# Keeping the low halves of weight blocks in DRAM between the two token halves of a two-block transformer kernel

## Chip, cores and metric

The kernel runs on one NeuronCore of a Trainium2 chip. The metric is the device time of one execution in microseconds, as the median of several runs. Engine names are those of the profile: PE (TensorE, with PEld for its weight loads), DVE (VectorE), ACT (ScalarE), POOL (GpSimd), SP (SyncE, which here only issues transfers).

## What is computed

512 tokens of width 1024 go through two blocks of a transformer, in float32. The first block has two layers: layer 0 is pooling beside latent attention, layer 1 is differential attention; each is followed by a SwiGLU feed-forward of width 2816. The second block has a mixer (stick-breaking attention, a gated linear recurrence, attention to a memory) and an expert layer that picks 16 experts per head for 8 heads. Cut to what matters here:

```python
def swiglu(h, w_gate, w_up, w_down):                 # D_MODEL 1024, D_FF 2816
    return (jax.nn.silu(h @ w_gate) * (h @ w_up)) @ w_down

def peer_ffn(h, w_query, sub_keys, expert_u, expert_v):
    q = (x_blk @ w_query).reshape(b, t, PEER_HEADS, 2, HALF_KEY)    # 1024 x 2048 weights
    scores = jnp.einsum('bthcd,hcnd->bthcn', q, sub_keys)
    top_s, top_i = lax.top_k(scores, PEER_TOPK)
    ...

# first block, layer 1:   h = h + diff_block(...);  h = h + swiglu(rmsnorm(h), ...)
# second block:           x = x + mixed @ w_out;    x = x + peer_ffn(rms_norm(x), ...)
```

## The kernel before

Every product is made of three matmuls (`mm3`, lines 268 to 271). A float32 operand is split into a high part, rounded to the matmul's format, and a low part, the rest. The three matmuls take high by high (line 269), high weight by low input (line 270) and low weight by high input (line 271), and add up in PSUM. `split` (lines 230 to 232) makes the two parts: ACT copies into the rounded format (line 231), and DVE or POOL subtracts (line 232).

`load_w` (lines 247 to 266) brings a weight block of 1024 x 256 in two parts of 128 partitions x 1024 columns: a transfer on SP's queue into `raw` (line 256, three buffers), then the split into `whi` and `wlo` (three buffers each). A second list, `LO`, says which engine subtracts each of the two parts. `low(n)` (lines 243 to 245) sets it: 0 means DVE for both parts, 2 means POOL for both, 1 means POOL for the first and DVE for the second. A part's buffers come free when its matmuls have run; the order of buffers follows the order of the program.

In the feed-forward of layer 1 the tokens are processed in two halves of 256, by two generators made by `ffn1` (lines 922 to 958): `ffn_a` for the first half and `ffn_b` for the second. Both load and split the same weights anew through `ffn` (lines 502 to 548): 11 gate blocks (line 527), 11 up blocks (line 530) and 12 down blocks (line 538; in the last of three rounds a part is 768 columns wide). The 8 query blocks of the expert layer (`queries`, line 1434) are likewise loaded for each half, in `PA.queries()` and `PB.queries()`.

The order around the change is written by hand at lines 1352 to 1361, 1720 to 1730 and 1763 to 1767, with generators that run side by side at given rates; a list scheduler then orders each engine's instructions by a model of time, so that an engine's queue is not simply the program's order. In time the stages are:

- 830 to 1047 us: `ffn_a` beside `memory()`, with `low(LO_A)`, which is `low(0)`.
- 1047 to 1134 us: projections of the first half for the mixer, with `low(2)`.
- 1134 to 1320 us: the mixer of the first half beside `ffn_b`, with `low(2)`. The mixer's recurrence (lines 1146 to 1226) alternates small DVE products with small matmuls (line 1170).
- 1320 to 1560 us: the mixer's output, `PA.queries()` beside the rest of `ffn_b`, with `low(2)`, then `low(LO_Z)`, which is `low(1)`, for the end of `ffn_b` (from about 1500 us) and the projections of the second half. `route` and `decode` (lines 1449 to 1512) run top-16 searches and one-hot products on DVE.
- 1560 to 1770 us: the mixer of the second half.
- 1770 to 2085 us: `PB.queries()` beside scores against expert rows (`scores`, line 1620, which also uses `load_w`) and gathers of expert rows by POOL-issued transfers (line 1516), whose scores DVE makes (line 1530), with `low(LO_P)`, which is `low(1)`.
- 2085 us to the end: the rest of the scores and the experts' sum.

The instructions that the prediction's steps touch are the subtraction at line 232, the ACT copy at line 231, the transfer at line 256, the matmul at line 271 that needs the low part, and on DVE lines 1479, 1496 and 1499 (`route` and `decode`).

Of the kernel before, what the change touches and what calls it, by code (L numbers as in the profile page):

```python
# [9 lines left out]
F = mybir.dt.float32  # L10
FR = mybir.dt.float32r
# [3 lines left out]
AF = mybir.ActivationFunctionType  # L15
# [6 lines left out]
S, D, KT = 512, 1024, 8  # L22
# [9 lines left out]
RB, WB = 3, 3  # L32
U2, UZ, UD = 3, 3, 4
LO_A, LO_Y, LO_M, LO_Z, LO_P = 0, 2, 2, 1, 1
# [18 lines left out]
F_1, F_2, F_3, F_4, L_4 = 1, 36, 2, 20, 1  # L53
# [114 lines left out]
def interleave(*gens):  # L168
    for _ in side_by_side(*gens):
        pass  # L170


def alongside(main, *others):

    live = [[g, n, 0] for g, n in (main,) + others]
    while True:
        e = min(live, key=lambda e: e[2] / e[1])
        e[2] += 1
        try:
            next(e[0])  # L180
        except StopIteration:
            if e[0] is main[0]:
                return
            live.remove(e)
# [7 lines left out]
def build(tc, A, out, stop=None, dump=None):  # L192
    nc = tc.nc
    V, SC, PE, GP = nc.vector, nc.scalar, nc.tensor, nc.gpsimd
    ctx = ExitStack()
    with ctx:
# [4 lines left out]
        tmps = ExitStack()  # L201
        tmp = tmps.enter_context(tc.tile_pool(name="tmp", bufs=2))
        psum = ctx.enter_context(tc.tile_pool(name="psum", bufs=8, space=PSUM))

        def ps(w=S):
            t = psum.tile([128, S], F, name="ps")
# [23 lines left out]
        def split(hi, lo, src, eng=V):  # L230
            SC.activation(hi, src, AF.Copy)  # L231
            eng.tensor_sub(lo, src, hi.bitcast(F))  # L232
# [10 lines left out]
        def low(n):  # L243

            LO[:] = [GP] * n + [V] * (2 - n)

        def load_w(ap, kt, eng=LO):

            n = ap.shape[1]
            w = n // kt  # L250
            half = (kt + 1) // 2
            parts = []
            for i, (a, b) in enumerate(((0, half), (half, kt))):
                c = (b - a) * w
                raw = wp.tile([128, 1024], F, name="raw", bufs=RB)[:, :c]
                nc.sync.dma_start(raw, ap[:, a * w:b * w])
                hi = wp.tile([128, 1024], FR, name="whi", bufs=WB)[:, :c]
                lo = wp.tile([128, 1024], FR, name="wlo", bufs=WB)[:, :c]
                split(hi, lo, raw, eng[i])
                parts.append((hi, lo))  # L260

            def get(k):
                hi, lo = parts[k >= half]
                k -= half if k >= half else 0
                return hi[:, k * w:(k + 1) * w], lo[:, k * w:(k + 1) * w]
            return get
# [235 lines left out]
        def ffn(l, nm, xh, xl, w, sl_, ah, al, stile, after):  # L502

            for r, (f0, nf, kd) in enumerate(FF_ROUNDS[l]):
                a_hi, a_lo = ah(), al()
                gates = []

                def gate_out(p):
                    s = stile()
                    V.tensor_mul(s, p, nm.R)  # L510
                    i = SC.activation(s, s, AF.Silu)
                    gates.append(s)
                    if MIXING[0] and len(gates) % 2 == 0:
                        in_order(i)
                        exp_ln()

                def up_out(f):
                    def ev(p):
                        u = stile()
                        V.tensor_mul(u, p, nm.R)  # L520
                        V.tensor_mul(u, u, gates.pop(0))
                        split(a_hi(f), a_lo(f), u)
                    return ev

                def items():
                    for c in range(nf // 2):
                        wg = load_w(A["w_gate%d" % l][f0 // 2 + c], KT)
                        yield lambda: feat_mm(ps(w), wg, 0, xh, xl), gate_out, True
                        yield lambda: feat_mm(ps(w), wg, 1, xh, xl), gate_out
                        wu = load_w(A["w_up%d" % l][f0 // 2 + c], KT)  # L530
                        yield lambda: feat_mm(ps(w), wu, 0, xh, xl), up_out(2 * c), True
                        yield lambda: feat_mm(ps(w), wu, 1, xh, xl), up_out(2 * c + 1)

                yield from steps(items(), {H_F[l][0]: [nm.roots], H_F[l][1]: [nm.rows]} if r == 0 else {})
                for c in range(4):
                    pp = [ps(w) for _ in range(2)]
                    for q in range(nf // kd):
                        wd = load_w(A["w_down%d%d" % (l, r)][c, q], kd)
                        for m in range(2):
                            for k in range(kd):  # L540
                                h, lo = wd(k)
                                f, mc = q * kd + k, slice(m * 128, m * 128 + 128)
                                mm3(pp[m], h[:, mc], lo[:, mc], a_hi(f), a_lo(f), f == 0, f == nf - 1)
                            yield
                    for m in range(2):
                        V.tensor_add(X[:, 2 * c + m, sl_], X[:, 2 * c + m, sl_], pp[m])
                    if r == len(FF_ROUNDS[l]) - 1:
                        after(2 * c + 2)
# [801 lines left out]
            between_inner(h.q0)  # L1350

        low(LO_A)
        interleave((ffn_a, 36), (memory(), 24))
        low(LO_Y)
        alongside((projections(HA), 16), (ffn_b, F_1))
        open_mix()
# [20 lines left out]
        hp = hps.enter_context(tc.tile_pool(name="rows", bufs=1, side="right"))  # L1377
        routes = ExitStack()
        RP = {}
        dram = ctx.enter_context(tc.tile_pool(name="dram", bufs=1, space=bass.MemoryType.DRAM))  # L1380
        Gd = dram.tile([4 * NV, 128, 128, 32], F, name="Gd")
        Sd = [dram.tile([128, 4, 128 * NV], F, name="Sd%d" % g) for g in range(NU)]

# [24 lines left out]
        class Peer:  # L1408
# [20 lines left out]
            def queries(self):  # L1429
                rp = RP[0] = routes.enter_context(tc.tile_pool(name="route", bufs=1, side="right"))  # L1430
                qs = {}
                for hd in range(9):
                    if hd < 8:
                        w = load_w(A["w_query"][hd], KT)
                        qs[hd] = rp.tile([128, 2, W], F, name="qh", bufs=2)
                        pp = [feat_mm(ps(W), w, m, self.xh, self.xl) for m in range(2)]
                        yield
                        for m in range(2):
                            SC.activation(qs[hd][:, m], pp[m], AF.Copy)
                        yield  # L1440
                    if hd == 0:
                        for t in range(self.ng):
                            self.rows(t)
                            yield
                    if hd >= 1:
                        yield from self.route(hd - 1, qs[hd - 1])
                routes.close()
# [272 lines left out]
        gather_a = gathered()  # L1720

        alongside((normed(0, W, xh, xl), 20), (ffn_b, F_3))
        alongside((PA.queries(), 112), (ffn_b, F_4), (gather_a, L_4))
        low(LO_Z)
        for _ in ffn_b:
            pass
        HB = Half(W, big)
        ring[0] = fixed_ring(UZ)
        open_mix()
# [73 lines left out]
```

## Time and profile before

| | |
|---|---|
| median of three runs | 3046.31 us (3045.76 to 10148.63) |
| the profiled execution's own time | 3051.8 us |
| its span | 3050.0 us |
| PE busy | 2886.0 us (95%) |
| DVE busy | 2142.5 us (70%) |
| ACT busy | 1375.8 us (45%) |
| POOL busy | 1155.7 us (38%) |
| granted PE clock, mean | 0.977 |

One execution is profiled, and all durations are from it. "Busy" is the time in which an engine has an instruction; a busy PE may still be waiting inside for weights. The granted clock is a share of full speed. In a row of a group, `out<-in` names what is written and read, `xN` is how many instructions there are, and after the bar stand the time busy and the mean of one in ns. In the waits, the first name waited for the second: us in total, times, longest.

### The profile page before, as it was taken

How to read it: one execution, taken by the hardware profiler on the slowest of the kernel's cores; microseconds unless marked ns; L12 is line 12 of the kernel's file. 1: busy time of each engine (PE TensorE's matmuls, PEld its weight loads, DVE VectorE, ACT ScalarE, POOL GpSimd, SP SyncE). 2: the span in 40 equal slices, each digit the busy share in tenths (PEclk: the TensorE clock that was granted, in tenths of full speed). 3: DMA queues.
4: the chain of work that ended last, by engine and by line, in shares of the span. 5: the costliest groups of instructions: out<-in, count | busy, mean ns of one | idle time of the engine just before them, and what ended most of it. 6: DMA issues, size and time to landing. Idle time of an engine off the chain costs nothing.

```text
span 3050.0 us, 44591 instructions
## 1 busy us (share of the span) xinstructions
PE 2886.0 (95%) x16770; PEld 2540.1 (83%) x16770; DVE 2142.5 (70%) x3877; ACT 1375.8 (45%) x2363; POOL 1155.7 (38%) x718
## 2 busy tenths in 40 slices
PE   8999999999999998889789989989999999899999
PEld 6568888878799998789786688889999998777887
DVE  6854344498776628659975668998787758788753
ACT  4533223477454545444354433337666643333332
POOL 3110000344310285468453146654554534444200
PEclk9999999999999999999899989999999999999999
DMA  3122232321255543245342157777877889999964
GB/s 134 41 77 97 87 107 85 101 70 42 59 179 180 173 159 105 84 137 182 114 153 74 39 197 279 252 261 290 301 287 282 299 318 387 363 373 380 340 224 145
DMA packets 195881, 568.29 MB, mean 186 GB/s; under 512 B 16944, under 2 KB 68528, under 8 KB 194000
## 3 DMA queue, kind: packets, MB, share of 16 engines
q1 hardware_dynamic: 157664, 427.61, 40.4%
q0 software_dynamic: 37712, 137.71, 12.1%
q8 instruction: 132, 2.16, 0.3%
q14 instruction: 85, 0.70, 0.1%
q10 hardware_dynamic: 288, 0.11, 0.0%
HBM read 512.93 MB, written 52.43 MB: 185 GB/s over the span
## 4 chain that ended last, share of the span: by engine, by line
PE 68%; DVE 18%; DMA 6%; ACT 3%; issue 3%; POOL 2%; SPq 0%; ACTq 0%; DVEq 0%; POOLq 0%
PE ps L269 14%; PE ps L271 14%; PE ps L270 14%; PE ps L1682 5%; PE ps L1683 5%; PE ps L1681 5%; PE ps L1563 3%; DVE wlo L232 2%; DMA raw<-in_peer_v_dram 2%; DMA u<-in_peer_u_dram,ix 2%; DVE u L1530 1%; POOL wlo L232 1%; PE ps L487 1%; PE ps L1170 1%; DVE nm L457 1%
## 5 line engine op out<-in xcount | busy, mean ns | idle before, releaser
L232 POOL TENSOR_TENSOR wlo<-raw,whi 128x1024 fp32r<-128x1024 f32 (+2 forms) x236 | 589.2, 2506 | 585.9 <-ACT whi L231 547.8
L231 ACT ACTIVATE whi<-raw 128x1024 fp32r<-128x1024 f32 (+2 forms) x518 | 515.6, 997 | 629.8 <-PE ps L270 344.3
L232 DVE TENSOR_TENSOR wlo<-raw,whi 128x1024 fp32r<-128x1024 f32 (+3 forms) x282 | 357.3, 1269 | 217.2 <-ACT whi L231 212.5
L271 PE MATMUL ps<-yh,wlo 128*128 128x384 f32 (+1 forms) x1152 | 386.0, 336 | 30.3 <-DVE wlo L232 30.2
L269 PE MATMUL ps<-yh,whi 128*128 128x384 f32 (+1 forms) x1152 | 389.8, 339 | 0.0
L270 PE MATMUL ps<-yl,whi 128*128 128x384 f32 (+1 forms) x1152 | 384.2, 334 | 0.0
L1682 PE MATMUL ps<-vl,gh 128*128 128x512 f32 x768 | 302.5, 394 | 3.7 <-DVE vl L232 3.5
L1683 PE MATMUL ps<-vh,gl 128*128 128x512 f32 x768 | 300.8, 392 | 0.0
L269 PE MATMUL ps<-XH,whi 128*128 128x512 f32 (+1 forms) x680 | 270.3, 402 | 8.6 <-ACT whi L231 8.6
L1516 POOL DMA_INDIRECT u<-in_peer_v_dram,ix x128 | 197.3, 1541 | 203.5 <-DVE h L1595 179.0
L270 PE MATMUL ps<-XL,whi 128*128 128x512 f32 (+1 forms) x680 | 267.1, 395 | 0.0
L271 PE MATMUL ps<-XH,wlo 128*128 128x512 f32 (+1 forms) x680 | 262.7, 395 | 1.8 <-DVE wlo L232 1.8
L1681 PE MATMUL ps<-vh,gh 128*128 128x512 f32 x768 | 240.3, 393 | 9.2 <-ACT vh L231 9.2
L271 PEld LDWEIGHTS ps<-yh,wlo 128*128 128x128 f32 x1152 | 219.7, 191 | 35.1 <-DVE wlo L232 35.1
L231 ACT ACTIVATE vh<-raw 128x1024 fp32r<-128x1024 f32 x128 | 133.2, 1055 | 249.7 <-DMA raw<-in_peer_v_dram 174.1
L1530 DVE SCALAR_TENSOR_TENSOR u<-u,h 128x1024 f32<-128x1024 f32 x127 | 185.3, 1465 | 52.3 <-DMA u<-in_peer_u_dram,ix 52.2
L270 PEld LDWEIGHTS ps<-yl,whi 128*128 128x128 f32 x1152 | 220.3, 191 | 0.0
L269 PEld LDWEIGHTS ps<-yh,whi 128*128 128x128 f32 x1152 | 220.1, 191 | 0.0
L369 POOL TENSOR_TENSOR sqa<-sqa,sq 128x512 f32<-128x512 f32 (+1 forms) x28 | 42.5, 1518 | 439.3 <-ACT sq L367 438.4
L269 PE MATMUL ps<-fx,whi 128*128 128x256 f32 x704 | 201.3, 289 | 6.2 <-ACT fx L353 4.4
L271 PE MATMUL ps<-fx,wlo 128*128 128x256 f32 x704 | 196.1, 287 | 5.9 <-DVE wlo L232 3.3
L232 DVE TENSOR_TENSOR vl<-raw,vh 128x1024 fp32r<-128x1024 f32 x128 | 155.3, 1222 | 65.6 <-ACT vh L231 65.2
(428 smaller groups left out, 7124.3 us busy)
## 6 DMA issues: line engine op xcount, KB each, us to landing
raw<-in_uT_dram SPq DMA_DIRECT2D x128, 512.0 KB, 6.0
raw<-in_peer_v_dram SPq DMA_DIRECT2D x128, 512.0 KB, 6.8
raw<-in_w_gate_dram SPq DMA_DIRECT2D x66, 512.0 KB, 3.7
raw<-in_w_up_dram SPq DMA_DIRECT2D x66, 512.0 KB, 3.8
raw<-in_w_in_dram SPq DMA_DIRECT2D x52, 512.0 KB, 3.7
Sd<-s SPq DMA_DIRECT2D x32, 768.0 KB, 6.4
Gd<-st SPq DMA_DIRECT2D x12, 2048.0 KB, 10.5
gt<-Gd SPq DMA_DIRECT2D x32, 768.0 KB, 8.7
```

The costliest lines, as they stand in the source:

```text
L231: SC.activation(hi, src, AF.Copy)
L232: eng.tensor_sub(lo, src, hi.bitcast(F))
L269: PE.matmul(out, wh, xh, start=first, stop=False)
L270: PE.matmul(out, wh, xl, start=False, stop=False)
L271: PE.matmul(out, wl, xh, start=False, stop=last)
L369: GP.tensor_add(self.acc, self.acc, q)
L1516: i = GP.indirect_dma_start(out=u, out_offset=None, in_=A[table], in_offset=bass.IndirectOffsetOnAxis(ap=self.idx[t, hd][:, j:j + 1], axis=0))
L1530: V.scalar_tensor_tensor(u, u, 1.0, self.h2[t], op0=OP.mult, op1=OP.mult, accum_out=self.sd[t][:, hd, j:j + 1])
L1563: PE.matmul(p[:, n * 128:(n + 1) * 128], q[:, n], e[:, n], start=True, stop=True)
L1681: PE.matmul(p, gh[:, e, ts], h[:, cs], start=False, stop=False, skip_group_check=True)
L1682: PE.matmul(p, gh[:, e, ts], l[:, cs], start=False, stop=False, skip_group_check=True)
L1683: PE.matmul(p, gl[:, e, ts], h[:, cs], start=False, stop=end, skip_group_check=True)
```

## The change

In `ffn_a` and in `PA.queries()` the low part of the second half (`i == 1`) of each block is written into a buffer of a pool of its own, three deep, and stored from there to a DRAM tensor by a transfer that POOL issues. In `ffn_b` and in `PB.queries()` the low part of that half is not computed: a transfer on SP's queue loads it from DRAM into a `wlo` buffer, and ACT makes the high part from `raw` as before. Layer 0 and all other weights keep the old way. The numbers: 34 feed-forward and 8 query parts are stored once and loaded once.

```diff
-        def load_w(ap, kt, eng=LO):
+        KEPT, KEEP = {}, [None]
+        def load_w(ap, kt, eng=LO, key=None):
...
                 hi = wp.tile([128, 1024], FR, name="whi", bufs=WB)[:, :c]
-                lo = wp.tile([128, 1024], FR, name="wlo", bufs=WB)[:, :c]
-                split(hi, lo, raw, eng[i])
+                keep = i == 1 and key is not None
+                first = keep and key not in KEPT
+                lo = (KEEP[0]() if first else wp.tile([128, 1024], FR, name="wlo", bufs=WB))[:, :c]
+                if keep and not first:
+                    nc.sync.dma_start(lo.bitcast(F), KEPT[key])
+                    SC.activation(hi, raw, AF.Copy)
+                else:
+                    split(hi, lo, raw, eng[i])
+                if first:
+                    KEPT[key] = dram.tile([128, c], F, name="kept%d" % len(KEPT))
+                    nc.gpsimd.dma_start(KEPT[key], lo.bitcast(F))
...
-                        wg = load_w(A["w_gate%d" % l][f0 // 2 + c], KT)
+                        wg = load_w(A["w_gate%d" % l][f0 // 2 + c], KT, key=("gate", f0 // 2 + c) if l else None)
-                        wu = load_w(A["w_up%d" % l][f0 // 2 + c], KT)
+                        wu = load_w(A["w_up%d" % l][f0 // 2 + c], KT, key=("up", f0 // 2 + c) if l else None)
-                        wd = load_w(A["w_down%d%d" % (l, r)][c, q], kd)
+                        wd = load_w(A["w_down%d%d" % (l, r)][c, q], kd, key=("down", r, c, q) if l else None)
...
-        interleave((ffn_a, 36), (memory(), 24))
+        with tc.tile_pool(name="kept", bufs=1) as kp:
+            KEEP[0] = lambda: kp.tile([128, 1024], FR, name="kl", bufs=3)
+            interleave((ffn_a, 36), (memory(), 24))
...
-                        w = load_w(A["w_query"][hd], KT)
+                        w = load_w(A["w_query"][hd], KT, key=("query", hd))
...
-        alongside((PA.queries(), 112), (ffn_b, F_4), (gather_a, L_4))
-        low(LO_Z)
-        for _ in ffn_b:
-            pass
+        with tc.tile_pool(name="kept2", bufs=1) as kp:
+            KEEP[0] = lambda: kp.tile([128, 1024], FR, name="kl", bufs=3)
+            alongside((PA.queries(), 112), (ffn_b, F_4), (gather_a, L_4))
+            low(LO_Z)
+            for _ in ffn_b:
+                pass
```

The DRAM pool, which was opened after the first mixer, is opened at the start.

## Rows read from the trace of the kernel before

**Rows 1.** Busy time of each engine by stage (us; windows A:B, length first)

```profile
core 0: us, PE busy (x) PEld busy (x) DVE busy (x) ACT busy (x) POOL busy (x), PEclk, DMA share, GB/s
830.00:1047.00 217.00, 211.24 (x1716) 207.54 (x1716) 150.05 (x262) 109.70 (x172) 22.62 (x31) 0.98 0.54 179
1134.00:1320.00 186.00, 167.28 (x1227) 150.43 (x1226) 130.80 (x340) 90.11 (x157) 100.44 (x68) 0.94 0.30 102
1320.00:1440.00 120.00, 113.68 (x947) 113.22 (x946) 83.26 (x265) 55.84 (x88) 86.74 (x36) 0.96 0.49 166
1440.00:1560.00 120.00, 92.33 (x673) 88.25 (x672) 119.72 (x311) 45.62 (x77) 72.63 (x47) 0.89 0.37 123
1770.00:2085.00 315.00, 284.12 (x1725) 279.15 (x1725) 280.56 (x662) 124.03 (x211) 185.08 (x103) 0.97 0.72 255
2085.00:2500.00 415.00, 414.07 (x2628) 413.65 (x2628) 311.44 (x350) 260.00 (x598) 202.32 (x112) 1.00 0.81 297
```

**Rows 2.** What PE waited for: 1134:1320 (one row), 1440:1560 (two), 1770:2085 (one)

```profile
PE ps L1170 <- DVE PT L1175: 10.2, 3, 5.3
...
PE ps L271 <- DVE wlo L232: 7.8, 4, 3.3
PE ps L271 <- POOL wlo L232: 6.4, 6, 2.0
...
PE ps L271 <- DVE wlo L232: 30.2, 16, 4.4
```

**Rows 3.** Timeline around 1440 us: POOL (first row) and DVE (start, us, instruction)

```profile
1438.99 8.77 POOL L232 TENSOR_TENSOR wlo<-raw,whi 128x1024 fp32r<-128x1024 f32 x3 [0.75 <-ACT whi L231]
...
1439.74 2.39 DVE L1499 CAST af<-ai 128x64 f32<-128x64 int32 x1
```

**Rows 4.** Groups by shape, 1400:1560: DVE (four rows), then POOL (one)

```profile
L1479 DVE TENSOR_TENSOR cand<-ts 128x256 f32<-128x256 f32 x13 | 14.0, 1077 | 0.0
...
L1496 DVE TENSOR_SCALAR ai<-bp 128x64 int32<-128x64 int32 x8 | 8.3, 1038 | 0.0
L1499 DVE CAST af<-ai 128x64 f32<-128x64 int32 x8 | 8.0, 1000 | 0.0
...
L232 DVE TENSOR_TENSOR wlo<-raw,whi 128x768 fp32r<-128x768 f32 x4 | 4.3, 1072 | 0.0
...
L232 POOL TENSOR_TENSOR wlo<-raw,whi 128x1024 fp32r<-128x1024 f32 x31 | 80.2, 2604 | 30.4 <-ACT whi L231 30.3
```

**Rows 5.** The same DVE lines in 1830:2085 (first row: ns min/median/max of line 1479)

```profile
L1479 DVE TENSOR_TENSOR cand<-ts x14: 397/400/2336, 1847.5 to 2043.4; 128x256 f32<-128x256 f32 x14
...
L1496 DVE TENSOR_SCALAR ai<-bp 128x64 int32<-128x64 int32 x8 | 1.6, 204 | 0.0
L1499 DVE CAST af<-ai 128x64 f32<-128x64 int32 x8 | 1.5, 183 | 0.0
```

**Rows 6.** Groups by shape on DVE, 1740:1975, where the second half's query blocks run

```profile
L1530 DVE SCALAR_TENSOR_TENSOR u<-u,h 128x1024 f32<-128x1024 f32 x44 | 60.8, 1386 | 23.3 <-DMA u<-in_peer_u_dram,ix 23.3
L232 DVE TENSOR_TENSOR wlo<-raw,whi 128x1024 fp32r<-128x1024 f32 x25 | 46.1, 1845 | 10.9 <-ACT whi L231 7.0 <-PE ps L270 3.8
```

**Rows 7.** Landing times: query (1740:1975), gate (1400:1560), gate (860:1040), expert rows (2100:2400)

```profile
DMA to landing us min/median/max: 3.9/5.2/8.7
...
raw<-in_w_gate_dram SPq DMA_DIRECT2D x6, 512.0 KB, 4.1
...
raw<-in_w_gate_dram SPq DMA_DIRECT2D x19, 512.0 KB, 4.6
...
raw<-in_uT_dram SPq DMA_DIRECT2D x57, 512.0 KB, 6.0
```

**Rows 8.** SP's queue in the first half's feed-forward: the pace of blocks

```profile
923.58 1.79 SPq L256 DMA_DIRECT2D raw<-in_w_gate_dram  x2
...
934.91 1.79 SPq L256 DMA_DIRECT2D raw<-in_w_gate_dram  x2
```

**Rows 9.** A plain transfer issued by POOL, ns min/median/max on POOL

```profile
L1045 POOL DMA_DIRECT2D m<-in_memT_dram x1: 536/536/536, 837.7 to 837.7; - x1
```

More of the change, by code (lines that the diff above doesn't have):

```diff
@@ L203, in build @@
         psum = ctx.enter_context(tc.tile_pool(name="psum", bufs=8, space=PSUM))
+        dram = ctx.enter_context(tc.tile_pool(name="dram", bufs=1, space=bass.MemoryType.DRAM))
         def ps(w=S):
@@ L1379, in build @@
         RP = {}
-        dram = ctx.enter_context(tc.tile_pool(name="dram", bufs=1, space=bass.MemoryType.DRAM))
         Gd = dram.tile([4 * NV, 128, 128, 32], F, name="Gd")
```

## Prediction

> **What bounds the kernel now.** I read the page first, for the engines' shares: PE is busy 95% of the span, so anything that does not fill PE's gaps is worth nothing. Then busy time by stage [rows 1], to find the gaps in the stages that the change touches, and then PE's waits in those stages [rows 2], to see who makes them. The reader is to see three kinds of stage. In 830 to 1047 PE is busy 211.2 of 217 us, with POOL at 22.6: PE sets the pace. In 1134 to 1320 PE lacks 186.0 - 167.3 = 18.7 us, and its longest wait (10.2 us) is for small DVE copies of the recurrence, not for low parts. In 1440 to 1560 DVE is busy 119.7 of 120 us and PE lacks 27.7: DVE sets the pace. In 1770 to 2085 PE lacks 30.9 us, and 30.2 of it is one row, the wait for low parts that DVE makes. After 2085 PE is full (414.1 of 415), and nothing of the change is there. So all that this change can win lies in 18.7 + 27.7 + 30.9 = 77.3 us of PE gaps, and in 1320 to 1440, where PE lacks 6.3 us.
>
> Last I read single DVE instructions beside POOL's, since the change takes work from both. A cast of 64 columns took 2.39 us while POOL was subtracting low parts [rows 3]; in a later stage it takes 0.18 [rows 5]. In 1400 to 1560, with 31 of POOL's full-size subtractions, lines 1479, 1496 and 1499 have means of 1077, 1038 and 1000 ns [rows 4]; in that later stage they take 400 (median), 204 and 183. The excess is 13 x 0.68 + 8 x 0.83 + 8 x 0.82 = 22.0 us, or 22.0 / 31 = 0.71 us of DVE per POOL subtraction. This is why low parts on POOL are not free.
>
> **What is removed.** Of the second half's 34 feed-forward low parts, I count the transfers on SP's queue: 15 are in 1134 to 1320 and 6 in 1320 to 1400, on POOL; 9 more come after 1400 on POOL; the last 4, of 768 columns, are on DVE. The 8 query parts are on DVE.
>
> *1440 to 1560.* 9 x 0.71 = 6.4 us of DVE freed by POOL, and 4 x 1.07 = 4.3 us of DVE's own subtractions [rows 4], 10.7 us where DVE is never idle. Some of it turns into waits for other things (ACT, transfers): I take 8 us; the ends are 0 and the gap of 27.7.
>
> *1134 to 1320.* 15 x 0.71 = 10.7 us of DVE. DVE is busy 70% here and only its recurrence products are on the path, so I take 4 us; the ends are 0 and 18.7. In 1320 to 1440 I take nothing: PE is 95% busy; at most 6.3.
>
> *1770 to 2085.* 8 x 1.845 = 14.8 us of DVE [rows 6]. A third (8 of 25) of the low parts of 1740 to 1975 go, while the wait for DVE's low parts is 30.2 us in all; the gathers' products (line 1530, 60.8 us busy and 23.3 idle for the gather ahead of them) stay in front of the others. A third of 30.2 is 10; I take 9; the ends are 0 and 14.8.
>
> **What is added.** *34 + 8 stores.* POOL's issue of a plain transfer is 0.54 us [rows 9], so 34 x 0.54 = 18 us on a POOL that is busy 22.6 of 217 us, hidden by idle time. POOL's queue stands at each store until DVE has made the part; behind it wait the sums of squares for the memory's norm and, at the end of `ffn_a`, for the next projections. The trace does not show a store beside these loads. At 34 x 0.5 MB in 217 us, the traffic rises from 179 to about 260 GB/s; near that rate (297 GB/s) the same size of load lands in 6.0 us instead of 4.6 [rows 1, 7], with PE still full. The extra 1.4 us falls on loads that are issued a block or more ahead, so from 0 to 34 x 1.4 = 48 us if no lead were left; I take 0 by the row at 297 GB/s, and 2 us for the last stores, which stand ahead of POOL's sums at 1047. Nor do I expect the store's buffer to be late: three buffers at 5.7 us a block give 17 us. In the query stage 8 x 0.54 = 4 us on POOL (86.7 of 120 busy) is less than the subtractions that leave it.
>
> *42 loads of low parts.* A load waits on SP's queue for a `wlo` buffer, and the `raw` loads of the next block are behind it; ACT waits for those and PE for ACT. Two blocks take 934.91 - 923.58 = 11.3 us [rows 8], 5.7 us each. The buffer for the second part comes free at three quarters of one block and is wanted at a quarter of the next: 2.8 us. A load of this size lands in 4.1 us [rows 7], so it is 1.3 us late where blocks follow each other without a break. The way it replaces, ACT's copy and then POOL's 2.6 us [rows 4], does not fit into 2.8 us either; I take it as half as late. That leaves 0.65 us more in the 9 blocks after 1440, 6 us; some falls where DVE is late anyway, so I take 3, between 0 and 9 x 1.3 = 12. Where blocks alternate with other work (21 blocks before 1400) I take 0. For the query blocks, which alternate with score blocks, I take 0, with 8 x 5.2 = 42 us [rows 7] as the upper end if nothing of the landing is covered; the lower end is 0.
>
> **Sum.** -8 - 4 - 9 + 2 + 3 = -16 us. The profiled execution took 3051.8 us (span 3050.0 and 1.8 around it), so 3035.8 for one like it; the median is 5.5 lower, 3046.3, and gives 3030.
>
> **The rivals.**
>
> *Hidden anyway.* PE's gaps are refilled by the next wait: in 1770 to 2085 the remaining 17 DVE low parts wait behind the same gathers, and in 1440 to 1560 the searches end when they did. For it: 23.3 us of DVE's idle time there is for gathers, not for work. Against: DVE is full in 1440 to 1560. Then only about 3 us are won: 3043.
>
> *Slower: the loads come late.* One mechanism: in SP's queue a low-part load stands until PE frees its buffer, and the landing is then uncovered. It decides from the point where the time between a buffer's release and its use is shorter than the landing time: 2.8 against 4.1 us after 1440, and in the query blocks wherever the load's issue waits for the score matmuls ahead. Price: 9 x 1.3 = 12 and 8 x 5.2 = 42 us, with the gains of 21 us and the 2 us for the stores: +35, 3081. For it: the query landing reaches 8.7 us at most [rows 7]. Against: SP's order is made by a schedule that can put other loads first, and the buffers have a score half of slack.
>
> *The whole subtraction is given back.* Each POOL subtraction costs DVE its whole 2.6 us where DVE is the bound: 9 x 2.6 + 4.3 = 27.7 us, just the gap of 1440 to 1560; the 18.7 us of 1134 to 1320 go as well (15 x 2.6 = 39), and 14.8 us in the query stage; with 5 us of costs -56: 2990. For it: single instructions are stretched by 2.2 us [rows 3, 5]. Against: the mean is 0.71. [...]
>
> **How the numbers follow.** Chances: forecast 0.50, hidden anyway 0.23, late loads 0.18, the whole given back 0.09. The forecast's own range, with its costs and gains moved by half, is 3015 to 3045. For eight in ten I go from 3000, which leaves out most of the last rival, to 3070, which takes in "hidden" and half of the late loads, where the query part is half covered. A measurement of this kernel can tell about 2%, 61 us, from no change. Faster by more (under 2985) needs the last rival and a little more: 0.04. Slower by more (over 3107) needs the late loads and 1.1 us for each of the other 25 loads: 0.04. Within 2%: 0.92.
>
> **What would show it.** Right: DVE's subtractions in 1740 to 1975 fall from 25 to about 17, PE's wait for them from 30 to about 20 us; lines 1496 and 1499 get shorter means in 1400 to 1560, and PE lacks about 20 us there; 830 to 1047 keeps its length. Wrong: a wait of PE's line 271 for the low-part load of over 10 us, or raw loads that land no later but are issued later; or a longer `ffn_a` with ACT waiting for `raw`. If PE's gaps after 1440 keep their sum although DVE is lighter, the gain was hidden.

## The result and the profile after

The changed kernel takes 3028.39 us (median of 6 runs, 3021.53 to 3031.74), against 3046.03 us for the kernel before (median of 6). The ratio is 0.9934, with an interval of 0.9918 to 0.9949: 0.5 to 0.8% faster, by the ratio 0.0066 x 3046 = 20 us. One run of the kernel before, of 10148.63 us, is not in the ratio. The profiled execution of the changed kernel took 3024.55 us (span 3022.7). It lies near the fast end of its runs, and the one of before (3051.8) near the slow end of its own, so the two profiles differ by 27.3 us where the medians differ by 17.6. A second profile of the changed kernel, taken later, took 3034.15 us; where a stage's gain is given below, both stand.

Some lines have moved: 232 (the subtraction) is 233 here, 271 (the matmul with the low part) is 285, 1170 is 1184, 1175 is 1189, 1185 is 1199, 1187 is 1201, 1189 is 1203, 1194 is 1208, 1196 is 1210, 1479 is 1494, 1496 is 1511, 1499 is 1514, 1530 is 1545, 1563 is 1578, 1577 is 1592. Line 267 loads a kept part, line 273 stores one.

Busy time by stage in the changed kernel, columns as in [rows 1]; the first two rows are stretches of [rows 1] by the clock (the first is 1 us longer), the others are the same work, which comes earlier here:

```profile
core 0: us, PE busy (x) PEld busy (x) DVE busy (x) ACT busy (x) POOL busy (x), PEclk, DMA share, GB/s
830.00:1048.00 218.00, 212.13 (x1725) 207.90 (x1724) 151.32 (x262) 110.93 (x174) 37.76 (x54) 0.98 0.77 255
...
1134.00:1320.00 186.00, 179.80 (x1396) 163.91 (x1395) 113.76 (x348) 100.02 (x167) 79.91 (x59) 0.98 0.49 168
...
1420.00:1502.00 82.00, 68.95 (x565) 67.35 (x563) 82.00 (x254) 33.83 (x54) 34.70 (x16) 0.94 0.64 214
1502.00:1537.00 35.00, 23.36 (x150) 21.61 (x150) 33.49 (x46) 15.34 (x26) 29.11 (x30) 0.85 0.39 134
...
1747.00:2051.00 304.00, 282.10 (x1730) 278.24 (x1729) 272.54 (x657) 124.82 (x214) 175.40 (x103) 0.97 0.79 277
2051.00:2473.00 422.00, 417.05 (x2629) 415.54 (x2629) 312.96 (x349) 257.86 (x596) 205.66 (x111) 1.00 0.80 292
```

The second row is the one to look at. In the same 186 us PE did 1396 matmuls instead of 1227; its gap went from 18.7 to 186.0 - 179.8 = 6.2 us, and the granted clock rose from 0.94 to 0.98 [rows 1]. Between 1420 and 1502 DVE is still full, 82.00 of 82 us. The query stage (1747 to 2051) has about the same 1730 matmuls as before and is 11 us shorter. The stretch after it is 422 us instead of 415 for the same 2629 matmuls: 7 us are lost again there. PE's busy time holds waits for weights as well: in the kernel before each of the 16 matmuls of line 271 that waited for DVE's parts [rows 2] began together with its own weight load, and the first of them, at 1783.07 us, took 0.44 us where the next matmuls of its shape took 0.34.

To size the stages by something that both kernels do, I take the first and last issue of three weights on SP's queue. First the kernel before, then the changed one (count, ns min/median/max, first and last start in us):

```profile
L256 SPq DMA_DIRECT2D raw<-in_w_in_dram x52: 327/328/383, 1046.8 to 1609.7; - x52
L256 SPq DMA_DIRECT2D raw<-in_w_out_dram x16: 327/328/388, 1299.6 to 1743.4; - x16
L256 SPq DMA_DIRECT2D raw<-in_uT_dram x128: 327/328/1086, 1749.8 to 2473.1; - x128
```

```profile
L261 SPq DMA_DIRECT2D raw<-in_w_in_dram x52: 327/328/384, 1047.6 to 1585.2; - x52
L261 SPq DMA_DIRECT2D raw<-in_w_out_dram x16: 327/328/328, 1281.0 to 1720.4; - x16
L261 SPq DMA_DIRECT2D raw<-in_uT_dram x128: 327/328/1386, 1726.6 to 2445.1; - x128
```

The differences of these numbers, for both profiles of the changed kernel and for the experiments:

| us | to the first `w_in` | first `w_in` to first `w_out` | first `w_out` to last `w_out` | last `w_out` to last `uT` |
|---|---|---|---|---|
| before | 1046.8 | 252.8 | 443.8 | 729.7 |
| changed | 1047.6 | 233.4 | 439.4 | 724.7 |
| changed, second profile | 1050.1 | 231.6 | 438.9 | 731.0 |
| `e1_ring` | 1045.3 | 254.4 | 448.7 | 728.4 |
| `e2_ffn` | 1050.0 | 227.8 | 444.3 | 730.7 |
| `e3_query` | 1048.2 | 253.9 | 444.9 | 725.3 |
| `e4_dummy_sub` | 1049.9 | 255.2 | 448.9 | 724.3 |
| `e5_dummy_set` | 1050.0 | 247.9 | 439.8 | 719.3 |
| `e6_stores` | 1048.8 | 257.8 | 450.0 | 730.6 |
| `e7_dve` | 1042.0 | 241.7 | 452.0 | 728.0 |
| `e8_gate_both` | 1051.3 | 231.4 | 443.3 | 725.3 |
| `e9_load_dve` | 1050.0 | 230.7 | 440.1 | 730.4 |
| `e10_dve_both` | 1046.7 | 234.3 | 450.4 | 725.9 |

So the gain lies in the second column, the first mixer's stage beside the feed-forward blocks of the second half: 19.4 and 21.2 us in the two profiles. The third column gives 4 to 5 us, the last 5.0 or -1.3, and the first loses 1 to 3. The two profiles of the changed kernel differ by 1.8 us in the second column and by 6.3 in the last, so a few us in the last say nothing.

What PE waited for in the changed kernel: in the mixer stage (one row), in the query stage (two), behind it (one):

```profile
PE ps L1184 <- DVE PT L1189: 1.7, 1, 1.7
...
PE ps L285 <- DVE wlo L233: 14.2, 7, 4.0
PE ps L285 <- DMA wlo<-kept: 6.5, 4, 2.9
...
PE ps L1578 <- DVE oq L1592: 4.8, 2, 3.8
```

The wait for the recurrence's copies, 10.2 us before [rows 2], is 1.7. The wait for DVE's low parts in the query stage is 14.2 instead of 30.2 us, but 6.5 us of waits for loaded parts are new. Behind it PE waits 4.8 us for DVE in a stage that was full.

What changed on DVE in the mixer stage is seen in the recurrence's four products, each of two SBUF inputs, in 1134 to 1300 (busy us, mean ns, idle before), and in the durations of line 1189 (ns min/median/max). The kernel before:

```profile
L1185 DVE TENSOR_TENSOR hg_qs<-pj 128x128 f32<-128x128 f32 x30 | 16.5, 550 | 3.5 <-PE ps L1170 3.5
L1189 DVE TENSOR_TENSOR hg_ks<-hg_k,hg_s 128x128 f32<-128x128 f32 x28 | 16.3, 581 | 0.2 <-PE ps L1170 0.2
...
L1196 DVE TENSOR_TENSOR pj<-pj 128x128 f32<-128x128 f32 x26 | 11.1, 427 | 0.2
...
L1194 DVE TENSOR_TENSOR hg_s<-hg_s,pj 128x128 f32<-128x128 f32 x30 | 8.9, 302 | 0.0
...
L1189 DVE TENSOR_TENSOR hg_ks<-hg_k,hg_s x28: 273/284/2491, 1146.3 to 1266.5; 128x128 f32<-128x128 f32 x28
```

The changed one, in the same stretch:

```profile
L1208 DVE TENSOR_TENSOR hg_s<-hg_s,pj 128x128 f32<-128x128 f32 x30 | 17.1, 572 | 0.0
...
L1199 DVE TENSOR_TENSOR hg_qs<-pj 128x128 f32<-128x128 f32 x30 | 10.4, 347 | 2.9 <-PE ps L1184 2.8
L1203 DVE TENSOR_TENSOR hg_ks<-hg_k,hg_s 128x128 f32<-128x128 f32 x28 | 10.4, 370 | 0.2 <-PE ps L1184 0.2
...
L1210 DVE TENSOR_TENSOR pj<-pj 128x128 f32<-128x128 f32 x26 | 7.7, 295 | 0.2
```

Before the change the median of line 1189 is 284 ns and the longest 2491, about as long as one of POOL's subtractions. 24 of the 28 products are undisturbed (294 ns or less). The mean of 581 comes from the other four, of 2067 to 2491 ns: each of them began while POOL was in a subtraction, and ended 0.15 us after it. Where POOL makes both parts of a block one after the other, the pair can hold two products in turn, as in this piece of the kernel before (start, us, engine):

```profile
1199.23 4.74 POOL L232 TENSOR_TENSOR wlo<-raw,whi 128x1024 fp32r<-128x1024 f32 x2 [1.54 <-PE ps L1294]
...
1199.66 2.07 DVE L1189 TENSOR_TENSOR hg_ks<-hg_k,hg_s 128x128 f32<-128x128 f32 x1
1201.65 2.46 DVE L1185 TENSOR_TENSOR hg_qs<-pj 128x128 f32<-128x128 f32 x1
```

With fewer subtractions on POOL (22 instead of 32 in this stretch) the means of the two products that PE's next matmuls read, lines 1185 and 1189, fall by over a third. But line 1194 went the other way, from 302 to 572 ns: the subtractions that are left meet that product now. All four together got shorter by 7.2 us, from 52.8 to 45.6. For all DVE instructions I summed, from the two traces, what those that began in 1134 to 1300 during a subtraction of low parts took beyond the median of their line and shape: 35.7 us before (31 subtractions began there) and 22.4 after (21), 1.1 us for each subtraction in both.

The matmuls that take the products in, as a group of the same 1134 to 1300 and with their durations (ns min/median/max), before:

```profile
L1170 PE MATMUL ps<-hg_qs,hg_ks 128*128 128x128 f32 x112 | 19.9, 316 | 15.4 <-DVE PT L1175 10.2 <-DVE hg_ks L1189 5.2
...
L1170 PE MATMUL ps<-hg_qs,hg_ks x112: 270/275/552, 1144.8 to 1266.4; 128*128 128x128 f32 x112
```

and after:

```profile
L1184 PE MATMUL ps<-hg_qs,hg_ks 128*128 128x128 f32 x112 | 17.6, 290 | 3.2 <-DVE PT L1189 1.7 <-DVE hg_ks L1203 1.4
...
L1184 PE MATMUL ps<-hg_qs,hg_ks x112: 270/275/553, 1148.8 to 1251.1; 128*128 128x128 f32 x112
```

PE stood 15.4 us ahead of these 112 matmuls and stands 3.2 now. Their median is 275 ns in both kernels; the mean fell from 316 to 290 because fewer are longer than 300 ns, 14 instead of 31, with the higher mean clock.

### The profile page after: what moved, and what is told of

It is laid out like the page before. It is cut to its first block, busy times and chain, and to the rows that moved or that the text cites. A ratio compares the mean times of both kernels' runs of the same rounds, so it can differ in the third digit from the quotient of the medians.

```text
span 3022.7 us, 44731 instructions
## 1 busy us (share of the span) xinstructions
PE 2879.9 (95%) x16770; PEld 2535.8 (84%) x16770; DVE 2109.6 (70%) x3864; ACT 1375.9 (46%) x2363; POOL 1097.5 (36%) x731
## 4 chain that ended last, share of the span: by engine, by line
PE 68%; DVE 16%; DMA 8%; issue 3%; ACT 3%; POOL 2%; SPq 0%; DVEq 0%; ACTq 0%; POOLq 0%
PE ps L285 14%; PE ps L283 14%; PE ps L284 14%; PE ps L1697 5%; PE ps L1698 4%; PE ps L1696 4%; PE ps L1578 3%; DVE wlo L233 1%; DMA wlo<-kept 1%; DMA u<-in_peer_v_dram,ix 1%; DMA raw<-in_peer_v_dram 1%; PE ps L501 1%; DVE u L1545 1%; POOL wlo L233 1%; DMA u<-in_peer_u_dram,ix 1%
## 5 line engine op out<-in xcount | busy, mean ns | idle before, releaser
L232 ACT ACTIVATE whi<-raw 128x1024 fp32r<-128x1024 f32 (+2 forms) x476 | 472.4, 994 | 589.6 <-PE ps L284 311.5
L233 POOL TENSOR_TENSOR wlo<-raw,whi 128x1024 fp32r<-128x1024 f32 (+2 forms) x199 | 492.2, 2477 | 607.8 <-ACT whi L232 542.7
L233 DVE TENSOR_TENSOR wlo<-raw,whi 128x1024 fp32r<-128x1024 f32 (+3 forms) x235 | 285.0, 1214 | 206.1 <-ACT whi L232 205.7
L285 PE MATMUL ps<-yh,wlo 128*128 128x384 f32 (+1 forms) x1152 | 383.8, 335 | 21.5 <-DVE wlo L233 14.2
L1696 PE MATMUL ps<-vh,gh 128*128 128x512 f32 x768 | 244.0, 396 | 11.7 <-ACT vh L232 11.7
L283 PE MATMUL ps<-fx,whi 128*128 128x256 f32 x704 | 198.2, 284 | 11.3 <-ACT whi L232 8.5
L284 PE MATMUL ps<-fx,whi 128*128 128x256 f32 x704 | 196.0, 281 | 0.0
```

The lines of the kernel that those rows point to most:

```text
L283: PE.matmul(out, wh, xh, start=first, stop=False)
L284: PE.matmul(out, wh, xl, start=False, stop=False)
L285: PE.matmul(out, wl, xh, start=False, stop=last)
L1696: PE.matmul(p, gh[:, e, ts], h[:, cs], start=False, stop=False, skip_group_check=True)
```

## The experiments

All were timed in turns with the kernel before on the same chip, in three groups; the ratios are within a group. The kernel before had a median of 3047.75 us beside `e1_ring`, `e3_query`, `e4_dummy_sub` and `e5_dummy_set`, of 3049.4 beside `e2_ffn`, `e6_stores`, `e7_dve` and `e8_gate_both`, and of 3051.37 beside `e9_load_dve`, `e10_dve_both` and `e11_changed`, so times of different groups are compared by their ratios. None leaves out a part of the computation. Diffs are against the changed kernel, unless another is named.

**Is it POOL's reading?** Two kernels keep the whole change and give POOL back work of the length it lost, on a buffer that is not needed any more: once a subtraction that reads SBUF, once fills that only write it. Both hold the `raw` buffer until they are done, as the subtraction did before the change.

`e4_dummy_sub`:

```diff
                     SC.activation(hi, raw, AF.Copy)
+                    if eng[i] is GP:
+                        GP.tensor_sub(raw, raw, hi.bitcast(F))
```

> The changed kernel, and in the second pass POOL also subtracts the high part from the raw part, in place, for the 30 parts that it did before (the result is not used). All other work is as changed. If the gain of the mixer's stage and of the query stage of the first half comes from POOL's subtraction being gone, whether by its hold on DVE or by POOL's queue, 15 to 20 us come back: 3043 to 3048. If it comes from buffers or order, 3028 stays within 5. DVE's lines 1189, 1199, 1203 and 1514 should show means over 400 ns again.

Measured: 3056.6 us, ratio 1.0029 (1.0016 to 1.0042). The whole gain is gone, and more.

`e5_dummy_set`:

```diff
                     SC.activation(hi, raw, AF.Copy)
+                    if eng[i] is GP:
+                        GP.memset(raw, 0.0)
+                        GP.memset(raw, 1.0)
+                        GP.memset(raw[:, :512], 0.0)
```

> The same, but in place of the subtraction POOL fills the raw buffer with constants for about 2.5 us (two full fills and a half one), so it is as busy but reads nothing from SBUF. If POOL's subtraction hurts by blocking DVE's instructions with two inputs in SBUF, the time stays near the changed kernel's: 3028 to 3033. If it hurts by keeping the mixer's own POOL steps waiting in the queue, it is that of the kernel with the needless subtraction, 3043 to 3048.

Measured: 3035.0 us, ratio 0.9954 (0.9939 to 0.9968). Most of the gain stays. The groups of the same stretch, 1134 to 1300, on DVE and POOL, and the row by engine of 1134 to 1320, first in `e4_dummy_sub`:

```profile
L1205 DVE TENSOR_TENSOR hg_ks<-hg_k,hg_s 128x128 f32<-128x128 f32 x28 | 14.4, 515 | 0.2 <-PE ps L1186 0.2
...
L270 POOL TENSOR_TENSOR raw<-raw,whi 128x1024 f32<-128x1024 f32 x13 | 31.5, 2422 | 50.2 <-ACT whi L268 50.2
...
1134.00:1320.00 186.00, 164.78 (x1188) 146.97 (x1187) 127.74 (x330) 88.37 (x155) 99.45 (x67) 0.92 0.45 148
```

and in `e5_dummy_set`:

```profile
L1207 DVE TENSOR_TENSOR hg_ks<-hg_k,hg_s 128x128 f32<-128x128 f32 x28 | 8.0, 289 | 0.2 <-PE ps L1188 0.2
...
L271 POOL MEMSET raw<- 128x1024 f32 x15 | 14.3, 956 | 0.7
...
1134.00:1320.00 186.00, 171.94 (x1308) 155.06 (x1307) 116.55 (x343) 94.75 (x163) 108.57 (x101) 0.97 0.47 156
```

PE's longest wait in `e4_dummy_sub`, 1134 to 1320:

```profile
PE ps L1186 <- DVE PT L1191: 11.7, 3, 5.2
```

POOL is busier with the fills (108.6 us) than with the subtractions (99.5), yet the product takes 289 ns beside them against 515, the granted clock is 0.97 against 0.92, and PE did 120 matmuls more. With the subtractions the wait for `PT` is back at 11.7 us (10.2 before, [rows 2]); with the fills it is 3.1. What holds these products is not that POOL is busy: with the work that reads SBUF their mean is 515 ns, with the work that only writes it 289. The two kernels differ by 0.75%, 22 us of the median. From `e5_dummy_set` to the changed kernel there is 0.2% more, with intervals that overlap.

By stage the split is another one. In the second column of the table `e5_dummy_set` has 247.9 us, 7.3 less than `e4_dummy_sub` but still 14.5 more than the changed kernel. So in the mixer stage the larger part of the gain came back only when POOL's time and the `raw` buffer were free as well; which of the two it needs, no run separates. `e5_dummy_set` makes this up later: behind its last `w_out` it takes 1294.9 us, the shortest of all profiles (the two of the changed kernel: 1302.3 and 1311.5), although the fills are over by then; why is not shown.

The fills are not harmless to DVE either. Two copies with one input, which have a mean of 290 ns in 1134 to 1300 of the kernel before, stood here for two fills and ended 0.15 us after them (`e5_dummy_set`, start, us, engine):

```profile
1166.20 0.95 POOL L270 MEMSET raw<- 128x1024 f32 x1 [1.37 <-ACT whi L268]
...
1166.56 1.77 DVE L1049 COPY hn_b<-hn_r 128x256 f32<-128x256 f32 x2
1167.20 0.98 POOL L271 MEMSET raw<- 128x1024 f32 x1
```

One rival is left. A list scheduler orders each kernel's instructions anew, so these two differ a little in order too, and part of the 22 us may be order. Against that stands the whole set: the four kernels in which POOL reads for all 30 parts (`e1_ring`, `e3_query`, `e4_dummy_sub`, `e6_stores`) lie at ratios of 1.001 to 1.003, and the seven others at 0.992 to 0.997.

**Is it the buffers?** `e1_ring` has the new buffers `kl` and makes every low part twice, as before.

```diff
-                if keep and not first:
-                    nc.sync.dma_start(lo.bitcast(F), KEPT[key])
-                    SC.activation(hi, raw, AF.Copy)
-                else:
-                    split(hi, lo, raw, eng[i])
+                split(hi, lo, raw, eng[i])
                 if first:
-                    KEPT[key] = dram.tile([128, c], F, name="kept%d" % len(KEPT))
-                    nc.gpsimd.dma_start(KEPT[key], lo.bitcast(F))
+                    KEPT[key] = True
```

> The changed kernel with the buffers of the low parts kept apart in the first pass (three more buffers) but nothing stored or loaded: the second pass subtracts as before. If the gain comes from the work taken off POOL and DVE, the time is that of the kernel before, 3046 us within 6. If it comes from the three further buffers, it is that of the changed kernel, 3028. If it is an accident of the order of instructions, it may lie anywhere between.

Measured: 3053.65 us, ratio 1.0021 (1.001 to 1.0032). The buffers alone win nothing. They cost 0.2%; why, no run here shows.

**What do the stores cost?** `e6_stores` writes all 42 parts to DRAM and loads none of them.

```diff
-                if keep and not first:
-                    nc.sync.dma_start(lo.bitcast(F), KEPT[key])
-                    SC.activation(hi, raw, AF.Copy)
-                else:
-                    split(hi, lo, raw, eng[i])
+                split(hi, lo, raw, eng[i])
```

> The first pass stores all 42 parts, and nothing is loaded: the second pass subtracts as before. By the prediction the stores cost 2 us over the kernel whose only change is the further buffers (ratio 1.0021): 1.002 to 1.004. If the stores are what the kernel with the needless subtraction pays for (ratio 1.0029 although DVE has 12 parts less), 1.005 to 1.007, with the first half's feed-forward longer.

Measured: 3061.62 us, ratio 1.0034 (1.002 to 1.0047). Above `e1_ring` this is 0.13%, 4 us; the two intervals overlap, and the runs are of two groups.

**Which parts win?** `e2_ffn` keeps the 34 feed-forward parts alone, `e3_query` the 8 query parts alone.

```diff
-                        w = load_w(A["w_query"][hd], KT, key=("query", hd))
+                        w = load_w(A["w_query"][hd], KT)
```

> Only the 34 feed-forward parts are stored and loaded; the query blocks are as before. If the two halves of the change add up, the time is the changed kernel's less the 0.1% that the query half costs by itself: a ratio to the kernel before of 0.993, 3024 to 3027. If the query half helps only beside the feed-forward half (its 9 us of the prediction), it is 3034 to 3038.

Measured: 3033.98 us, ratio 0.994 (0.9918 to 0.9962), within its interval all of the changed kernel's gain.

For `e3_query` the same is done to the keys of the gate, up and down blocks:

```diff
-                        wg = load_w(A["w_gate%d" % l][f0 // 2 + c], KT, key=("gate", f0 // 2 + c) if l else None)
+                        wg = load_w(A["w_gate%d" % l][f0 // 2 + c], KT, key=("gate", f0 // 2 + c) if l > 1 else None)
```

> Only the 8 query parts are stored and loaded; the feed-forward is as before. By the prediction's step for the query stage it is 9 us under the kernel before, 3037, with PE's wait for DVE's low parts at about 20 us in place of 30. If the query stage's gain is hidden by gathers it is 3043 to 3049. If the whole gain lies there, 3028.

Measured: 3051.87 us, ratio 1.0011 (1.0 to 1.0021): no gain. Its row of the query stage by the clock of [rows 1], and PE's waits in it:

```profile
1770.00:2085.00 315.00, 291.14 (x1768) 287.83 (x1769) 278.33 (x681) 130.86 (x226) 178.60 (x104) 0.96 0.78 274
```

```profile
PE ps L285 <- DMA wlo<-kept: 11.1, 5, 3.9
PE ps L285 <- DVE wlo L233: 8.4, 4, 4.0
```

The wait for DVE's parts fell from 30.2 to 8.4 us, 11.1 us of waits for loaded parts came in its place, and by 2085 PE had done 1768 matmuls against 1725. Inside the stage there is a gain, and it is not in the time at the end. But this kernel has the query stage's new buffers too, and the buffers of both stages cost 0.2% in `e1_ring`; a gain of that size could be hidden under their cost.

**Is DRAM needed?** If POOL's reading is the cost, DVE can as well do that subtraction itself. `e7_dve` keeps nothing in DRAM; the second time, DVE subtracts the feed-forward's second parts.

```diff
-                lo = (KEEP[0]() if first else wp.tile([128, 1024], FR, name="wlo", bufs=WB))[:, :c]
-                if keep and not first:
-                    nc.sync.dma_start(lo.bitcast(F), KEPT[key])
-                    SC.activation(hi, raw, AF.Copy)
-                else:
-                    split(hi, lo, raw, eng[i])
+                lo = wp.tile([128, 1024], FR, name="wlo", bufs=WB)[:, :c]
+                split(hi, lo, raw, V if keep and not first else eng[i])
                 if first:
-                    KEPT[key] = dram.tile([128, c], F, name="kept%d" % len(KEPT))
-                    nc.gpsimd.dma_start(KEPT[key], lo.bitcast(F))
+                    KEPT[key] = True
...
-                        w = load_w(A["w_query"][hd], KT, key=("query", hd))
+                        w = load_w(A["w_query"][hd], KT)
```

> Nothing is stored or loaded. In the second pass of the feed-forward DVE subtracts the second part of every block itself, in place of POOL. If POOL's subtraction costs DVE as much as a subtraction of its own (about 1.2 us), DVE is no worse off and POOL's queue is free: 0.997 to 1.001. If only the removal of the work from both engines helps, DVE is 30 x 1.2 less 30 x 0.7 = 15 us worse off where it sets the pace: 1.002 to 1.006. If work on POOL is harmless it is slower by the 36 us of DVE: 1.008 to 1.012.

Measured: 3040.74 us, ratio 0.9971 (0.9958 to 0.9984). More work on DVE, and faster.

`e10_dve_both` is `e7_dve` with the first parts of those blocks on DVE too (the diff is against `e7_dve`):

```diff
-                split(hi, lo, raw, V if keep and not first else eng[i])
+                split(hi, lo, raw, V if key in KEPT else eng[i])
```

> Nothing is stored or loaded; in the second pass of the feed-forward DVE subtracts both parts. If POOL's hold on DVE is the whole cost and DVE has room, 0.993 to 0.996, and DRAM is not needed for the gain. If DVE's own work sets the pace, 68 x 1.2 = 82 us of it cannot be hidden in the gaps and the ratio is 0.998 or more.

Measured: 3035.46 us, ratio 0.9944 (0.9921 to 0.9966), without one byte in DRAM. The DVE groups of its 1134 to 1300, and its row by engine:

```profile
L233 DVE TENSOR_TENSOR wlo<-raw,whi 128x1024 fp32r<-128x1024 f32 x30 | 37.3, 1244 | 16.4 <-ACT whi L232 16.3
...
L1198 DVE TENSOR_TENSOR hg_ks<-hg_k,hg_s 128x128 f32<-128x128 f32 x28 | 8.2, 293 | 0.0
```

```profile
1134.00:1320.00 186.00, 177.41 (x1358) 159.52 (x1358) 129.03 (x377) 101.73 (x168) 41.15 (x42) 0.97 0.37 122
```

DVE makes a part in 1244 ns where POOL took 2.4 us, the product is back at 293 ns, and DVE's busy time in the stretch (129.0 us) is hardly below that of before (130.8, [rows 1]): 30 subtractions came onto it and the stretching went. PE has its work all the same. In the table, this kernel gains 18.5 us in the second column and loses 6.6 in the third, where `e1_ring` and `e4_dummy_sub` lose 5 as well; why is not shown.

`e9_load_dve` is `e2_ffn` (second parts from DRAM) with DVE for the first parts the second time:

```diff
                 else:
-                    split(hi, lo, raw, eng[i])
+                    split(hi, lo, raw, V if key in KEPT else eng[i])
...
-                        w = load_w(A["w_query"][hd], KT, key=("query", hd))
+                        w = load_w(A["w_query"][hd], KT)
```

> As the kernel with the feed-forward parts alone, and in the second pass the first part of each block, which is still computed, is subtracted by DVE in place of POOL, so that POOL subtracts nothing for the feed-forward there. If a POOL subtraction costs DVE more than DVE's own 1.2 us, as the move of the second parts to DVE suggests (30 of them, 0.3% faster), the other 30 give as much again: a ratio of 0.990 to 0.992. If DVE is by now the limit with its own work, it is 0.995 to 1.000.

Measured: 3030.57 us, ratio 0.9917 (0.9892 to 0.9942), the lowest ratio of all. In its query stage PE waits for DVE's low parts just as before, since nothing of the queries is kept:

```profile
PE ps L285 <- DVE wlo L233: 30.0, 16, 4.2
```

**Would more parts in DRAM win more?** `e8_gate_both` keeps the feed-forward's second parts and, of 11 gate blocks, the first part as well.

```diff
-                keep = i == 1 and key is not None
-                first = keep and key not in KEPT
-                lo = (KEEP[0]() if first else wp.tile([128, 1024], FR, name="wlo", bufs=WB))[:, :c]
+                keep = key is not None and (i == 1 or key[0] == "gate")
+                first = keep and (key, i) not in KEPT
+                lo = (KEEP[0]() if first and i else wp.tile([128, 1024], FR, name="wlo", bufs=WB))[:, :c]
...
```

> As the kernel with the feed-forward parts alone, and of the 11 gate blocks the first part too is stored and loaded: 11 subtractions less on POOL. If each is worth what the first 30 were (some 0.8 us), 9 us less than that kernel: a ratio of 0.990, 3016. If SP's queue or the traffic of 0.5 MB more per gate block is at its limit, it is slower than that kernel, 0.995 or more.

Measured: 3031.92 us, ratio 0.9941 (0.9919 to 0.9962): no more than `e2_ffn` (0.994). PE did 1405 matmuls in 1134 to 1320, against the 1396 of the changed kernel: that stage has little left to give. The 3016 us that was expected did not come.

**The changed kernel again**, in one group with `e9_load_dve` and `e10_dve_both`, as `e11_changed`:

> The changed kernel itself, beside the two others on one chip: a ratio of 0.993 within 0.002. If the query half is worth nothing beside the feed-forward half, it does not differ from the kernel with the feed-forward parts alone (0.994).

Measured: 3032.48 us, ratio 0.9933 (0.991 to 0.9956), as the first time. The intervals of `e9_load_dve`, `e10_dve_both` and this one overlap, so which of the three is fastest stays open.

## Why the prediction was right, and which of its terms were not

The forecast was 3030 us, and 3028.39 came. Direction, mechanism (POOL's subtractions stretch DVE's instructions) and sum were right. That the sum came so near is luck: by stage -5, -4 and -9 us were forecast, and about -5, -20 and nothing that can be told from zero came, with costs of 10 us in `e6_stores` against 2.

**The mixer stage, -4: the term that was mis-sized.** I counted 15 x 0.71 = 10.7 us of DVE and took 4, because DVE is busy only 70% there. It measured 19.4 and 21.2 us, just above the 18.7 that I had set as the end. Three things were missed. The 0.71 us came from three DVE lines of another stage; over all DVE instructions of this one it is 1.1 us for each subtraction. The recurrence is a chain between PE and DVE, so a stretched product delays the next step, however idle DVE is otherwise: PE's idle time ahead of the recurrence's matmuls fell from 15.4 to 3.2 us, and in it the wait for `PT`, which I had read as "not for low parts", from 10.2 to 1.7 us. It was a wait for low parts, at one remove: `PT` came late because DVE stood for POOL, as `e4_dummy_sub` shows, where the wait returns with the reading. And my upper end was PE's gap, which takes the clock as given: with fewer gaps the granted clock rose from 0.94 to 0.98, and the recurrence's matmuls went from a mean of 316 to 290 ns. How the 20 us split between what POOL reads and the time that it takes is not settled: by `e4_dummy_sub` and `e5_dummy_set` the reading alone is 7.3 us of this column.

**1440 to 1560, -8, with +3 for late loads: the size came, its cause is not shown.** The work of 120 us takes 82 + 35 = 117 in the changed kernel, the third column gives 4.4 and 4.9 us, and -5 was forecast for both terms. But `e2_ffn`, with the same feed-forward parts loaded, has 444.3 us in that column, 0.5 more than before, and `e1_ring`, which loads none, 448.7: kernels differ there by as much as the gain. DVE's groups in 1380 to 1537:

```profile
L1494 DVE TENSOR_TENSOR cand<-ts 128x256 f32<-128x256 f32 x14 | 12.4, 882 | 0.0
L1514 DVE CAST af<-ai 128x64 f32<-128x64 int32 x8 | 6.8, 849 | 0.0
L1511 DVE TENSOR_SCALAR ai<-bp 128x64 int32<-128x64 int32 x8 | 5.4, 672 | 0.0
```

Their means were 1077, 1000 and 1038 [rows 4]; in the later stage these lines take 400 (median), 183 and 204 [rows 5]. Less than half of the stretch is gone, since POOL still makes the first parts. The gap of PE is 11.6 + 13.0 = 24.7 us here, not the 20 that I named as a sign.

**The query stage, -9: failed at the end of the run, right inside the stage.** The signs that I named came. DVE's subtractions in 1717 to 1952 (1740 to 1975 before) are 18 instead of 25, and PE's wait is 14.2 + 6.5 = 20.7 instead of 30.2 us:

```profile
L1545 DVE SCALAR_TENSOR_TENSOR u<-u,h 128x1024 f32<-128x1024 f32 x46 | 62.4, 1358 | 19.2 <-DMA u<-in_peer_u_dram,ix 19.2
L233 DVE TENSOR_TENSOR wlo<-raw,whi 128x1024 fp32r<-128x1024 f32 x18 | 24.6, 1367 | 12.7 <-ACT whi L232 12.7
```

The stage is 11 us shorter. But the step "after 2085 PE is full, and nothing of the change is there" failed: the same 2629 matmuls then take 422 us instead of 415, and PE waits 4.8 us for DVE there. In time the query parts, with their buffers and stores, are worth nothing that can be told from zero: `e3_query` stands at 1.0011, and `e2_ffn` without them within 0.1% of the changed kernel. What exactly is late after 2051 was not tried.

**Costs, +2 and +3: too small.** The stage up to the first `w_in` grew by 0.8 and 3.3 us, as forecast for it. But buffers and stores together cost 0.34% in `e6_stores`, 10 us. Two thirds of it are already in `e1_ring`, which moves nothing: a cost that I had not listed. The stores and loads by themselves:

```profile
L273 POOL DMA_DIRECT2D kept<-kl x42: 531/533/574, 850.0 to 1451.9; - x42
L267 SPq DMA_DIRECT2D wlo<-kept x42: 326/327/1587, 1145.7 to 1933.3; - x42
...
  DVE kl L233: 152.9, 30
...
  PE ps L285: 10.6, 8
```

POOL issues a store in 533 ns, as [rows 9] had it, and waits 152.9 us in all for DVE's parts, in a stage where it has little else to do. PE waited for a loaded part 8 times, 10.6 us. I had named a wait of over 10 us as a sign against me. It came, but in the query stage, where 6.5 us of it lie, it stands in place of longer waits for parts made on the chip: both together are 20.7 us there against 30.2.

**The ledger by runs.** From `e1_ring` over `e6_stores`, `e4_dummy_sub` and `e5_dummy_set` to the changed kernel, the differences of the ratios times 3046 us:

| step | us |
|---|---|
| the new buffers | +6.4 |
| 42 stores | +4.0 |
| loads, and 12 subtractions less on DVE | -1.5 |
| 30 subtractions on POOL, which read SBUF, turned into fills | -22.8 |
| the fills in their place gone | -6.1 |
| sum | -20.1 |

Each step has an interval of some 0.2%, 6 us, and they are of two groups, so only the fourth row is far from zero by itself. The profiles split the fourth and fifth rows otherwise (7.3 and 14.5 us in the mixer stage), so it is their sum that is safe: 28.9 us for 30 subtractions, 0.96 us each, between my 0.71 and the 2.4 us of the whole instruction.

**The rivals.** *Hidden anyway* holds for the query stage alone, as far as `e3_query` can tell. *The loads come late*: they were late (6.5 us in the query stage), but nowhere near the 42, and the kernel is not slower. *The whole subtraction is given back*: 0.96 of 2.4 us each. For a single instruction it is right: a product of line 1189 took 2491 ns, where the median is 284. But of the 31 subtractions that began in 1134 to 1300 of the kernel before, 18 held a DVE instruction for more than 1 us, and PE waited ahead of the recurrence's matmuls only five times (15.4 us).

## What to carry to other kernels

Work that was handed to an idle POOL was not free here: the 30 subtractions, which read SBUF, were worth 28.9 us of the run, 0.96 us each. Look at the longest and the median duration of DVE's instructions beside such work (2491 and 284 ns for line 1189), and ask whether those DVE instructions are links in a chain with PE, not whether DVE is busy. Before building a way around such work (here through DRAM, with 42 stores and loads), try moving it to the engine it disturbs: DVE took 1244 ns for a part here and POOL 2415 (means of 1134 to 1300), and `e10_dve_both` has a gain that cannot be told from the changed kernel's, for a few edited lines. A stage that gets shorter counts only if the next one does not get longer, so read the gain at the last common event of both kernels.

## What was not expected of the hardware

Taking subtractions off POOL and onto DVE (32 of them, 39.8 us, in 1134 to 1320 of `e10_dve_both`) left DVE's busy time there as it was (129.0 against 130.8 us): what DVE's instructions took beyond their medians during subtractions on POOL fell from 41.3 to 2.2 us, as much as came. And the fills on POOL, beside which the product of two inputs had a mean of 289 ns, held copies with one input until they ended: two fills of 0.95 and 0.98 us held two copies for 1.77 us in all.
